# A second pool for the low parts of the weights, with 64 bytes ahead of those that stand as stationary operands

## The chip, the cores and the metric

One core of a Trainium2 chip runs the whole program in one launch. The metric is the device time of one execution in microseconds (us); less is better. Matrix products run on TensorE (PE in the rows; PEld is its loading of the stationary operand), evacuations and splits on VectorE (DVE) and ScalarE (ACT), transfers of weights are issued by SyncE (SP).

## The reference

One decoder layer on 256 tokens of 1024 channels in float32: a half-step SwiGLU block, a mixer (causal attention with 8 heads beside a short gated convolution, both from one input projection) and a second half-step SwiGLU block, each followed by a layer norm. Nearly all of the work is products of the 256 tokens with large weights.

```python
def swiglu(x, w_up, w_down):
    gate, up = jnp.split(x @ w_up, 2, axis=-1)          # w_up 1024 x 5632
    return (jax.nn.silu(gate) * up) @ w_down            # w_down 2816 x 1024

def hybrid_mixer(x, w_in, b_gate, conv_w, conv_b, w_proj_attn, w_proj_conv, w_out):
    z = x @ w_in                                        # w_in 1024 x 8192
    q, k, v, h, g_b, g_c, gates = jnp.split(z, SPLITS, axis=-1)
    y_attn = moba_attention(heads(q), heads(k), heads(v)) @ w_proj_attn
    y_conv = (g_b * short_conv(g_c * h, conv_w, conv_b)) @ w_proj_conv
    gate_attn, gate_conv = jnp.split(jax.nn.sigmoid(gates + b_gate), 2, axis=-1)
    return (gate_attn * y_attn + gate_conv * y_conv) @ w_out

def reference(x, ...):
    x = layer_norm(ALPHA * x + 0.5 * swiglu(x, ffn1_w_up, ffn1_w_down), ln1_g, ln1_b)
    x = layer_norm(ALPHA * x + hybrid_mixer(x, ...), ln2_g, ln2_b)
    return layer_norm(ALPHA * x + 0.5 * swiglu(x, ffn2_w_up, ffn2_w_down), ln3_g, ln3_b)
```

## The kernel before

**Three products for one.** Every operand is kept as two parts in the type fp32r: a high part (the value rounded to fp32r) and a low part (the rest). A product is high times high, plus high times low, plus low times high. All matmuls of this kind come from one helper and stand under L117; the shape tells them apart.

**Units of weights.** The weights come in units of 128 x 2048 elements (1 MB). SP loads a unit into one of three `raw` buffers, ScalarE writes its high part (L883) and VectorE its low part (L886) into two `S` buffers; there are ten of them, 8192 bytes per partition each, taken in turn. The function `prep` does this, and `advance` decides when, from planned times of use; `now["t"]` is that plan's clock, and nothing in it is measured. The q and k of the attention take `S` buffers too (one each for four heads), and `state["hold"]` keeps room for them.

**Two ways to multiply.** In `rows` and `D` the activations stand as the stationary operand (128 x 128) and 512 columns of weights move, high or low. In `cols` the weights stand and the activations (tiles `X`, transposed, high and low parts beside each other) move. One call of `cols` takes one unit (`col_unit`: 1024 rows by 256 columns of a weight) and issues 32 matmuls: 16 *wide* ones, with 128 x 128 of the high part standing and 512 columns moving (the high and low part of 256 tokens at once), and 16 *narrow* ones, with 128 x 128 of the low part standing and 256 columns moving (the high part alone). They stand in this order, for the two banks 0 and 1 of the unit:

```python
            wide.append(mm(lambda b=b: box[b], lambda c=c: u.hi[:, c], ... 512, u))
            narrow.append(mm(lambda b=b: box[b][:, 0:256], lambda c=c: u.lo[:, c], ... 256, u))
    return add(wide[:KT + 1] + narrow + wide[KT + 1:])      # 9 wide, 16 narrow, 7 wide
```

There are 74 such units: 20 of the first SwiGLU block's up projection, 28 of the input projection (q, k, gates, h, gc, gb), 8 of the two projections behind the mixers, 18 of the second SwiGLU block. So there are 1184 narrow matmuls with a weight's low part standing. The rest of TensorE's work is 2038 matmuls of 512 columns in fp32r (1184 of them the wide ones of `cols`), some hundred of attention, and transposes (L190).

**Order.** The whole program is recorded in one fixed order per engine; nothing is decided on the chip. Every tile of the program begins, within a partition, at a remainder of 128 bytes to a multiple of 512, but the `N` tiles (activations of 128 x 1032) and the small vectors: an `N` tile is 4128 bytes long, so that the nine of them begin at 0, 32, 64 or 96 bytes behind a multiple of 128 (the one of the transposes at the start of the second SwiGLU block's tokens 128 to 255 begins at 64).

Of the kernel before, what the change touches and what calls it, by code (L numbers as in the profile page):

```python
# [9 lines left out]
F = mybir.dt.float32  # L10
R = mybir.dt.float32r
# [15 lines left out]
LEAD, LEAD0, LEAD1, PACE, DELAY, QUIET = 30.0, -1.0, 0.9, 2.2, 1.2, 4.0  # L27
OFF, AT0, AT1, AT2, HEAD = 5.0, 1.3, 10.5, 15.0, 7.5
AD1, AD2, AD3 = 2.0, 1.5, 1.0
S_BUFS, X_BUFS, RAW_BUFS, N_BUFS, T_BUFS, ACC_BUFS = 10, 3, 3, 9, 8, 8  # L30


class Op:
# [6 lines left out]
class Unit:  # L40


    def __init__(self, src, chunks=2):
        self.src, self.chunks = src, chunks
        self.raw = self.hi = self.lo = None
        self.left = 0


class Slots:


    def __init__(self, pool, tag, shape, bufs):
        self.pool, self.tag, self.shape, self.bufs, self.live, self.n = pool, tag, shape, bufs, 0, 0

    def get(self, dt=F):
        assert self.live < self.bufs, self.tag
        self.live += 1
        self.n += 1
        return self.pool.tile(self.shape, dt, tag=self.tag, name=f"{self.tag}{self.n}", bufs=self.bufs)

    def free(self, n=1):
        self.live -= n
# [3 lines left out]
def layer(ctx: ExitStack, tc: tile.TileContext, a: dict, out: bass.AP):  # L66
# [3 lines left out]
    ctx.enter_context(tc.manual_schedule())  # L70

    S = Slots(sb, "S", [128, 2048], S_BUFS)
    X = Slots(sb, "X", [128, 4096], X_BUFS)
    RAW = Slots(sb, "raw", [128, 2048], RAW_BUFS)
    N = Slots(sb, "N", [128, 1032], N_BUFS)
# [2 lines left out]

    base, ins, units, sig, st = [], [], [], [], {}
    now = {"t": 0.0}  # L80
    state = {"dma": 0, "prep": 0, "chunk": 0, "t": -100.0, "hold": 0, "quiet": 0.0}


    for pool in (S, X, RAW, T):
        pool.get()
        pool.free()

# [46 lines left out]

    pending = []

    def new_unit(src, chunks=2):
        u = Unit(src, chunks)
        units.append(u)
        return u  # L140

# [36 lines left out]
    def col_unit(w, c0):  # L178

        return new_unit(lambda raw: [(raw.rearrange("p (k n) -> p k n", k=KT),  # L180
                                      w[:, c0:c0 + 256].rearrange("(k p) n -> p k n", p=128))])

    def transposes(src, n, evac):

# [364 lines left out]
    def QK(kind, c):  # L549
        def epi(bank, j):  # L550
            if j == 0:
                state["hold"] -= 1
                st[kind, c] = S.get(R).rearrange("p (s h n) -> p s h n", s=2, h=4)
            t_ = T.get()
            both(t_[:, 0:256], bank)
            split_later(st[kind, c][:, 0, j], st[kind, c][:, 1, j], t_[:, 0:256], T.free)

        return four(kind, c, epi)
# [61 lines left out]
    def attention(head, at, dt):  # L620
        c, h = head // 4, head % 4
        box = {}
        qT = lambda s, lo, hi: st["q", c][:, s, h, lo:hi]
        kT = lambda s, lo, hi: st["k", c][:, s, h, lo:hi]

        def bank(name, lo, hi):
            def f():
                if name not in box:
                    box[name] = ACC.get()
                return box[name][:, lo:hi]  # L630
            return f


        both_k = lambda: st["k", c][:, :, h, 0:128]
        ops = [mm(bank("S", 0, 256), lambda: qT(0, 0, 128), both_k, True, False, 256),
               mm(bank("S", 0, 128), lambda: qT(1, 0, 128), lambda: kT(0, 0, 128), False, True, 128)]
        ops += passes(bank("S", 256, 512), lambda s: qT(s, 128, 256), lambda w: kT(w, 0, 256), True, True, 256)

        def softmax():
            if head == 0:  # L640
                st["xT", "a"] = xnew()
            P = T.get()
            b = box["S"]
            mx = small([128, 2], "mx")
            sm = small([128, 2], "sm")
            nc.vector.scalar_tensor_tensor(P[:, 0:128], b[:, 0:128], SCALE, mask, op0=OP.mult, op1=OP.add)
            nc.vector.scalar_tensor_tensor(P[:, 0:128], b[:, 128:256], SCALE, P[:, 0:128], op0=OP.mult, op1=OP.add)
            nc.vector.tensor_scalar(P[:, 128:256], b[:, 256:384], SCALE, None, op0=OP.mult)
            nc.vector.scalar_tensor_tensor(P[:, 256:384], b[:, 384:512], SCALE, mask, op0=OP.mult, op1=OP.add)
            ACC.free()  # L650
            nc.vector.reduce_max(mx[:, 0:1], P[:, 0:128], axis=mybir.AxisListType.X)
            nc.vector.reduce_max(mx[:, 1:2], P[:, 128:384], axis=mybir.AxisListType.X)
            nc.vector.tensor_scalar(mx, mx, -1.0, None, op0=OP.mult)

            def exps():
                nc.scalar.activation(P[:, 0:128], P[:, 0:128], AF.Exp, bias=mx[:, 0:1], accum_out=sm[:, 0:1])
                nc.scalar.activation(P[:, 128:384], P[:, 128:384], AF.Exp, bias=mx[:, 1:2], accum_out=sm[:, 1:2])
                defer(AD2, recip)

            def recip():  # L660
                nc.vector.reciprocal(sm, sm)
                defer(AD3, norm)

            def norm():
                nc.scalar.activation(P[:, 0:128], P[:, 0:128], AF.Identity, scale=sm[:, 0:1])
                nc.scalar.activation(P[:, 128:384], P[:, 128:384], AF.Identity, scale=sm[:, 1:2])

            defer(AD1, exps)
            box["P"] = P

        ops[-1].after.append(softmax)
        put(at, dt, ops)

        def evac(tb):
            T.free()
            box["PT"] = [T.get(R)[:, 0:2 * n].rearrange("p (s n) -> p s n", s=2) for n in (256, 128)]
            for pt, c0, n in zip(box["PT"], (0, 256), (256, 128)):
                split(pt[:, 0], pt[:, 1], tb[:, c0:c0 + n])

        put(at, dt + AT1, transposes(lambda i: box["P"][:, i * 128:(i + 1) * 128], 3, evac))  # L680


        v = lambda s, kt: st["v"][:, s, kt, head * 128:(head + 1) * 128]
        flat = lambda i: box["PT"][i].rearrange("p s n -> p (s n)")
        late = lambda: bank("O", 0, 512)().rearrange("p (s n) -> p s n", s=2)[:, :, 128:256]
        ops = [mm(bank("O", 0, 512), lambda: v(0, 0), lambda: flat(0), True, False, 512),
               mm(late, lambda: v(0, 1), lambda: box["PT"][1], False, False, 256),
               mm(bank("O", 0, 256), lambda: v(1, 0), lambda: box["PT"][0][:, 0], False, False, 256),
               mm(bank("O", 128, 256), lambda: v(1, 1), lambda: box["PT"][1][:, 0], False, True, 128)]

        def fin():
            aT = st["xT", "a"][:, head].rearrange("p s t n -> p s (t n)")
            T.free(2)
            o = T.get()[:, 0:256]
            both(o, box["O"])
            ACC.free()
            split_later(aT[:, 0], aT[:, 1], o, T.free)
            if h == 3:
                S.free(2)
            if head == NH - 1:  # L700
                X.free()

        ops[-1].after.append(fin)
        put(at, dt + AT2, ops)

    def hold():
        state["hold"] += 2

    for t in range(2):
        for c in range(2):  # L710
# [166 lines left out]

    def prep(u, c):
        if c == 0:
            u.hi, u.lo = S.get(R), S.get(R)  # L880
        w = 2048 // u.chunks
        s = slice(c * w, (c + 1) * w)
        nc.scalar.copy(u.hi[:, s], u.raw[:, s])  # L883

        def rest():
            nc.vector.tensor_tensor(u.lo[:, s], u.raw[:, s], u.hi[:, s].bitcast(F), op=OP.subtract)  # L886
            if c == u.chunks - 1:
                RAW.free()

        defer(DELAY if now["t"] > 12 else 0.0, rest, u)  # L890
# [7 lines left out]
    def advance(must=None):  # L898
        flush(must)
        while state["prep"] < len(order):  # L900
            load()
            u, c, t = order[state["prep"]], state["chunk"], now["t"]
            if must is None or pos[id(must)] < state["prep"]:
                if need[id(u)] + c * 2.6 / u.chunks > t + min(LEAD, LEAD0 + t * LEAD1):
                    break
                if t < state["t"] + PACE * 2 / u.chunks * min(1, 0.4 + t * 0.03):
                    break
                if t < state["quiet"]:
                    break
                if c == 0 and S.live + state["hold"] + 2 > S_BUFS:  # L910
                    break
            prep(u, c)
            state["t"] = t
            state["chunk"] += 1
            if state["chunk"] == u.chunks:
                state["prep"] += 1
                state["chunk"] = 0
        flush(must)

    load()  # L920
    for t, op in zip(clock, prog):
# [3 lines left out]
        if op.unit is not None:  # L925
            op.unit.left -= 1
            if op.unit.left == 0:
                S.free(2)
        for f in op.after:
            f()  # L930
    now["t"] = 1e9
    flush()
    assert not any(s.live for s in (S, X, RAW, T, ACC, N)), [(s.tag, s.live) for s in (S, X, RAW, T, ACC, N)]


_INS = ["x", "ffn1_w_up", "ffn1_w_down", "ln1_g", "ln1_b", "w_in", "b_gate", "conv_w", "conv_b",
# [19 lines left out]
```

## Time and profile before

| | |
|---|---|
| time, median of 3 runs | 643.73 us (643.54 to 643.81) |
| time of the profiled execution | 643.73 us |
| its span (first to last instruction) | 642.0 us |
| TensorE busy | 633.2 us, 99% of the span |
| TensorE's loads of stationary operands | 547.7 us, 85% |
| VectorE busy | 455.7 us, 71% |
| ScalarE busy | 357.1 us, 56% |
| mean traffic with HBM | 188 GB/s |

The profiled execution took as long as the median run, and 1.73 us of it lie outside its span. The busy times overlap: each engine works on its own queue, and waits for others by semaphores. Matmuls are pipelined, so that the busy times of single matmuls overlap too: the length of one record (some 280 or 390 ns) is not its cost; the distance from one matmul's start to the next one's is.

### The profile page before, as it was taken

Reading aid. Unit: us, or ns where it says so; the run is one execution under the profiler, and the core shown is the slowest. Engines: PE = TensorE matmul, PEld = TensorE weight load, DVE = VectorE, ACT = ScalarE, POOL = GpSimd, SP = SyncE. Lnnn points to the kernel's source line nnn. Section 1 sums busy time; section 2 is a strip of 40 time slices with the busy share of each in tenths; the row PEclk is TensorE's granted clock in tenths of the full one; section 3 lists DMA queues with packets and bytes.
Section 4 is the critical chain, followed back from the end, with each engine's and each line's share of the span. In section 5 each row is a group of like instructions: output and inputs, shape, how many; then the busy total and the mean of one; then the engine's idle time right before and its main releaser. Section 6 shows DMA issues by size and latency. Waiting matters only on the chain.

```text
span 642.0 us, 8774 instructions
## 1 busy us (share of the span) xinstructions
PE 633.2 (99%) x3416; PEld 547.7 (85%) x3416; DVE 455.7 (71%) x732; ACT 357.1 (56%) x624; POOL 18.5 (3%) x25
## 2 busy tenths in 40 slices
PE   9999999999999999999999999999999999999995
PEld 6888888888888888898888888888888888888884
DVE  4786666666678577778869987886966676666627
ACT  5665555555534458676698665552556655555510
POOL 2000000000011000000000000001100000000001
PEclk9999999999999999999999999999999999999998
DMA  9865665667645572555666655572666756556301
GB/s 295 267 226 198 211 236 193 210 212 260 193 126 171 165 230 90 155 174 158 203 212 192 224 200 189 198 253 75 196 197 201 259 196 197 197 196 197 132 1 66
DMA packets 95854, 121.18 MB, mean 189 GB/s; under 512 B 2196, under 2 KB 84548, under 8 KB 95812
## 3 DMA queue, kind: packets, MB, share of 16 engines
q1 hardware_dynamic: 95524, 120.23, 57.6%
q8 instruction: 27, 0.44, 0.3%
q10 hardware_dynamic: 288, 0.39, 0.2%
q14 instruction: 15, 0.12, 0.1%
HBM read 119.56 MB, written 1.05 MB: 188 GB/s over the span
## 4 chain that ended last, share of the span: by engine, by line
PE 98%; DVE 1%; issue 0%; DVEq 0%; ACT 0%; POOL 0%; POOLq 0%
PE acc L117 96%; PE acc L190 1%; PE acc L147 0%; DVE N L824 0%; DVEq L952 0%; DVE S L886 0%; DVE N L828 0%; ACT X L203 0%; POOL T L90 0%; DVE bn L240 0%; DVE N L238 0%; DVE mv L250 0%; PE acc L719 0%; DVE X L204 0%; DVEq L886 0%
## 5 line engine op out<-in xcount | busy, mean ns | idle before, releaser
L117 PE MATMUL acc<-X,S 128*128 128x256 f32 (+1 forms) x2368 | 420.0, 338 | 0.0
L117 PEld LDWEIGHTS acc<-X,S 128*128 128x128 f32 x2368 | 363.4, 190 | 46.9
L886 DVE TENSOR_TENSOR S<-raw,S 128x1024 fp32r<-128x1024 f32 (+1 forms) x224 | 268.3, 1207 | 47.3 <-ACT S L883 46.0
L883 ACT CAST S<-raw 128x1024 fp32r<-128x1024 f32 (+1 forms) x224 | 227.7, 1034 | 47.6 <-PE acc L117 42.9
L117 PE MATMUL acc<-S,T 128*128 128x512 f32 (+1 forms) x546 | 123.4, 383 | 0.0
L117 PEld LDWEIGHTS acc<-S,T 128*128 128x128 f32 x546 | 100.1, 188 | 19.8
L379 DVE TENSOR_TENSOR T<-T,acc 128x256 f32<-128x256 f32 x132 | 55.4, 420 | 80.1 <-ACT T L378 79.7
L378 ACT COPY T<-acc 128x256 f32<-128x256 f32 x132 | 49.0, 371 | 99.1 <-PE acc L117 99.1
L117 PE MATMUL acc<-S,X 128*128 128x512 f32 x336 | 80.4, 395 | 0.1
L117 PEld LDWEIGHTS acc<-S,X 128*128 128x128 f32 x336 | 62.3, 188 | 13.7 <-DVE S L886 0.7
L213 ACT CAST T<-T 128x256 fp32r<-128x256 f32 x38 | 15.5, 407 | 24.9 <-DVE T L430 24.6
L424 ACT ACTIVATE T<-T 128x256 f32<-128x256 f32 x38 | 15.9, 418 | 13.9 <-DVE T L379 13.9
L203 ACT CAST X<-acc 128x512 fp32r<-128x512 f32 x16 | 9.4, 588 | 22.7 <-PE acc L190 14.3
L252 POOL TENSOR_TENSOR rs<-mv,mhalf 128x1 f32<-128x1 f32 x6 | 6.2, 1036 | 459.7 <-DVE mv L250 459.7
L204 DVE TENSOR_TENSOR X<-acc,X 128x512 fp32r<-128x512 f32 x16 | 10.9, 687 | 12.0 <-ACT X L203 11.9
L238 DVE SCALAR_TENSOR_TENSOR N<-acc,N 128x512 f32<-128x512 f32 (+1 forms) x13 | 8.4, 646 | 15.2 <-PE acc L117 15.2
L208 DVE TENSOR_TENSOR T<-T,T 128x256 fp32r<-128x256 f32 x38 | 15.9, 419 | 1.9 <-ACT T L213 1.9
L430 DVE TENSOR_TENSOR T<-T 128x256 f32<-128x256 f32 x38 | 16.2, 425 | 1.3
L203 ACT CAST T<-acc 128x128 fp32r<-128x128 f32 (+1 forms) x28 | 8.2, 293 | 15.1 <-DVE T L204 13.7
L379 DVE TENSOR_TENSOR N<-N,acc 128x256 f32<-128x256 f32 x24 | 10.0, 416 | 5.6 <-ACT N L378 5.6
L213 ACT CAST X<-T 128x256 fp32r<-128x256 f32 x16 | 6.5, 407 | 12.1 <-DVE T L379 6.8
L204 DVE TENSOR_TENSOR T<-acc,T 128x128 fp32r<-128x128 f32 (+1 forms) x28 | 9.1, 327 | 5.4 <-ACT T L203 5.4
(70 smaller groups left out, 213.8 us busy)
## 6 DMA issues: line engine op xcount, KB each, us to landing
raw<-in_ffn_w_up SPq DMA_DIRECT2D x38, 1024.0 KB, 5.1
raw<-in_w_in SPq DMA_DIRECT2D x32, 1024.0 KB, 5.4
raw<-in_ffn_w_down SPq DMA_DIRECT2D x22, 1024.0 KB, 4.8
raw<-in_w_proj_attn SPq DMA_DIRECT2D x4, 1024.0 KB, 5.3
raw<-in_w_proj_conv SPq DMA_DIRECT2D x4, 1024.0 KB, 4.9
raw<-in_w_out SPq DMA_DIRECT2D x4, 1024.0 KB, 5.0
raw<-in_ffn_w_up SPq DMA_DIRECT2D x8, 512.0 KB, 4.8
raw<-in_ffn_w_up SPq DMA_DIRECT2D x8, 256.0 KB, 5.3
```

Of the source, the lines that this page charges most:

```text
L117: return Op(lambda: nc.tensor.matmul(dst(), lhsT=lhsT(), rhs=rhs(), start=start, stop=stop), cols, unit)
L203: nc.scalar.copy(hi, src)
L204: nc.vector.tensor_tensor(lo, src, hi.bitcast(F), op=OP.subtract)
L208: nc.vector.tensor_tensor(lo, src, hi.bitcast(F), op=OP.subtract)
L213: nc.scalar.copy(hi, src)
L238: nc.vector.scalar_tensor_tensor(y[:, c], src, scale, st["ax", t][:, c], op0=OP.mult, op1=OP.add)
L378: nc.scalar.copy(dst, bank[:, 256:512])
L379: nc.vector.tensor_tensor(dst, dst, bank[:, 0:256], op=OP.add)
L424: defer(0.8, lambda: nc.scalar.activation(g[:, 0:256], g[:, 0:256], AF.Silu))
L430: nc.vector.tensor_tensor(g[:, 0:256], g[:, 0:256], g[:, 256:512], op=OP.mult)
L883: nc.scalar.copy(u.hi[:, s], u.raw[:, s])
L886: nc.vector.tensor_tensor(u.lo[:, s], u.raw[:, s], u.hi[:, s].bitcast(F), op=OP.subtract)
```

## The change

The `S` buffers are divided: high parts (and q) stay in `S`, now with five buffers, and low parts (and k) go to a new pool `L` with five. An `L` buffer has 32 elements (128 bytes) more than an `S` buffer, and the low part of a unit from `col_unit` begins 16 elements (64 bytes) behind its start; other low parts, and k, begin at the start. The counts of held buffers are kept for q and k apart.

```diff
-S_BUFS, X_BUFS, RAW_BUFS, N_BUFS, T_BUFS, ACC_BUFS = 10, 3, 3, 9, 8, 8
+S_BUFS, X_BUFS, RAW_BUFS, N_BUFS, T_BUFS, ACC_BUFS = 5, 3, 3, 9, 8, 8
...
-    def __init__(self, src, chunks=2):
-        self.src, self.chunks = src, chunks
+    def __init__(self, src, chunks=2, skip=0):
+        self.src, self.chunks, self.skip = src, chunks, skip
...
-    def get(self, dt=F):
-        assert self.live < self.bufs, self.tag
+        self.room = room
+
+    def get(self, dt=F, skip=0):
+        assert self.live < self.bufs and skip <= self.room, self.tag
         self.live += 1
         self.n += 1
-        return self.pool.tile(self.shape, dt, tag=self.tag, name=f"{self.tag}{self.n}", bufs=self.bufs)
+        p, n = self.shape
+        t = self.pool.tile([p, n + self.room], dt, tag=self.tag, name=f"{self.tag}{self.n}", bufs=self.bufs)
+        return t[:, skip:skip + n] if self.room else t
...
     S = Slots(sb, "S", [128, 2048], S_BUFS)
+    L = Slots(sb, "L", [128, 2048], S_BUFS, 32)
...
         return new_unit(lambda raw: [(raw.rearrange("p (k n) -> p k n", k=KT),
-                                      w[:, c0:c0 + 256].rearrange("(k p) n -> p k n", p=128))])
+                                      w[:, c0:c0 + 256].rearrange("(k p) n -> p k n", p=128))], skip=16)
...
-                st[kind, c] = S.get(R).rearrange("p (s h n) -> p s h n", s=2, h=4)
+                st[kind, c] = (S if kind == "q" else L).get(R).rearrange("p (s h n) -> p s h n", s=2, h=4)
...
-            u.hi, u.lo = S.get(R), S.get(R)
+            u.hi, u.lo = S.get(R), L.get(R, u.skip)
...
-                if c == 0 and S.live + state["hold"] + 2 > S_BUFS:
+                if c == 0 and max(S.live + state["holdq"], L.live + state["holdk"]) >= S_BUFS:
```

No instruction is added, removed or moved: on every engine the same instructions stand in the same order with the same shapes (lines are ten further down, and buffer numbers one higher). TensorE's queue at one unit of the first SwiGLU block, before (`S_790` is the unit's high part, `S_791` its low part, `X_115` the activations, `acc` the two banks):

```order
L117 MATMUL acc_922<-X_115,S_790 128x512 x8
L117 MATMUL acc_932<-X_115,S_790 128x512
L117 MATMUL acc_922<-X_115,S_791 128x256 x8
L117 MATMUL acc_932<-X_115,S_791 128x256 x8
L117 MATMUL acc_932<-X_115,S_790 128x512 x7
```

The same place with the change:

```order
L127 MATMUL acc_923<-X_116,S_791 128x512 x8
L127 MATMUL acc_933<-X_116,S_791 128x512
L127 MATMUL acc_923<-X_116,L_792 128x256 x8
L127 MATMUL acc_933<-X_116,L_792 128x256 x8
L127 MATMUL acc_933<-X_116,S_791 128x512 x7
```

Only the buffer that the sixteen narrow matmuls load their stationary operand from has moved, to another address.

By the addresses of the two built programs, the low parts of `col_unit` begin at a remainder of 0 (before) and of 64 (after) to 128 bytes. Since `L` buffers are longer, everything behind them lies 640 bytes further: `X`, `T` and `raw` keep their remainder to 128, while against the `S` buffers, whose addresses stay, they are displaced by 128 to a multiple of 512; the five `L` buffers lie at 0, 128, 256 and 384 to it.

## Rows read from the trace of the kernel before

**Rows 1.** The page, part 1: engine, busy us, share, instructions.

```profile
PE 633.2 (99%) x3416; PEld 547.7 (85%) x3416; DVE 455.7 (71%) x732; ACT 357.1 (56%) x624; POOL 18.5 (3%) x25
```

**Rows 2.** TensorE's waits: engine, line, releaser: total us, times, longest us.

```profile
PE acc L147 <- POOL T L90: 1.3, 1, 1.3
```

**Rows 3.** TensorE's groups by shape, whole span: count | busy us, mean ns | idle.

```profile
L117 PE MATMUL acc<-X,S 128*128 128x512 f32 x1184 | 288.9, 392 | 0.0
L117 PE MATMUL acc<-X,S 128*128 128x256 f32 x1184 | 154.7, 283 | 0.0
L117 PE MATMUL acc<-S,T 128*128 128x512 f32 x510 | 119.1, 390 | 0.0
L117 PE MATMUL acc<-S,X 128*128 128x512 f32 x336 | 80.4, 395 | 0.1
```

**Rows 4.** Timeline around one unit: wide, narrow, next wide (start, length, count).

```profile
97.54 1.98 PE L117 MATMUL acc<-X,S 128*128 128x512 f32 x8
...
99.82 1.48 PE L117 MATMUL acc<-X,S 128*128 128x256 f32 x11
...
101.26 1.55 PE L117 MATMUL acc<-X,S 128*128 128x512 f32 x6
```

**Rows 5.** That unit's groups: first narrow, wides behind, wides ahead; loads for wides, narrows.

```profile
L117 PE MATMUL acc<-X,S 128*128 128x256 f32 x1 | 0.3, 277 | 0.0
...
L117 PE MATMUL acc<-X,S 128*128 128x512 f32 x2 | 0.6, 396 | 0.0
...
L117 PE MATMUL acc<-X,S 128*128 128x512 f32 x9 | 2.2, 389 | 0.0
...
L117 PEld LDWEIGHTS acc<-X,S 128*128 128x128 f32 x10 | 1.9, 188 | 0.4
...
L117 PEld LDWEIGHTS acc<-X,S 128*128 128x128 f32 x13 | 1.6, 192 | 0.0
```

**Rows 6.** Timeline: three narrow matmuls behind an attention step.

```profile
240.16 0.52 PE L117 MATMUL acc<-X,S 128*128 128x256 f32 x3
```

**Rows 7.** Timeline: transposes of an N tile and of a T tile; then their group.

```profile
458.87 0.60 PE L190 MATMUL acc<-ident,N 128*128 128x128 f32 x4
...
251.32 0.49 PE L190 MATMUL acc<-ident,T 128*128 128x128 f32 x3
...
L190 PE MATMUL acc<-ident,T 128*128 128x128 f32 x36 | 6.2, 272 | 0.0
```

**Rows 8.** Groups of the split on ScalarE and VectorE, with what ended their idle time.

```profile
L883 ACT CAST S<-raw 128x1024 fp32r<-128x1024 f32 x216 | 222.9, 1049 | 45.8 <-PE acc L117 42.9 <-DMA raw<-in_ffn_w_up 2.5 <-DMA raw<-in_w_in 0.4
...
L886 DVE TENSOR_TENSOR S<-raw,S 128x1024 fp32r<-128x1024 f32 x216 | 262.6, 1224 | 45.8 <-ACT S L883 44.6
```

**Rows 9.** Span and granted clock.

```profile
core 0: 642.0 us, clock 0.997
```

More of the change, by code (lines that the diff above doesn't have):

```diff
@@ L49, with __init__ @@
 class Slots:
-    def __init__(self, pool, tag, shape, bufs):
+    def __init__(self, pool, tag, shape, bufs, room=0):
         self.pool, self.tag, self.shape, self.bufs, self.live, self.n = pool, tag, shape, bufs, 0, 0
-    def get(self, dt=F):
-        assert self.live < self.bufs, self.tag
+        self.room = room
+    def get(self, dt=F, skip=0):
+        assert self.live < self.bufs and skip <= self.room, self.tag
         self.live += 1
         self.n += 1
-        return self.pool.tile(self.shape, dt, tag=self.tag, name=f"{self.tag}{self.n}", bufs=self.bufs)
+        p, n = self.shape
+        t = self.pool.tile([p, n + self.room], dt, tag=self.tag, name=f"{self.tag}{self.n}", bufs=self.bufs)
+        return t[:, skip:skip + n] if self.room else t
     def free(self, n=1):
@@ L80, in layer @@
     now = {"t": 0.0}
-    state = {"dma": 0, "prep": 0, "chunk": 0, "t": -100.0, "hold": 0, "quiet": 0.0}
-    for pool in (S, X, RAW, T):
+    state = {"dma": 0, "prep": 0, "chunk": 0, "t": -100.0, "holdq": 0, "holdk": 0, "quiet": 0.0}
+    for pool in (S, L, X, RAW, T):
         pool.get()
@@ L135, in layer, with new_unit @@
     pending = []
-    def new_unit(src, chunks=2):
-        u = Unit(src, chunks)
+    def new_unit(src, chunks=2, skip=0):
+        u = Unit(src, chunks, skip)
         units.append(u)
@@ L551, in epi @@
             if j == 0:
-                state["hold"] -= 1
-                st[kind, c] = S.get(R).rearrange("p (s h n) -> p s h n", s=2, h=4)
+                state["hold" + kind] -= 1
+                st[kind, c] = (S if kind == "q" else L).get(R).rearrange("p (s h n) -> p s h n", s=2, h=4)
             t_ = T.get()
@@ L698, in fin @@
             if h == 3:
-                S.free(2)
+                S.free()
+                L.free()
             if head == NH - 1:
@@ L706, in hold @@
     def hold():
-        state["hold"] += 2
+        state["holdq"] += 1
+        state["holdk"] += 1
     for t in range(2):
@@ L927, in layer @@
             if op.unit.left == 0:
-                S.free(2)
+                S.free()
+                L.free()
         for f in op.after:
@@ L932, in layer @@
     flush()
-    assert not any(s.live for s in (S, X, RAW, T, ACC, N)), [(s.tag, s.live) for s in (S, X, RAW, T, ACC, N)]
+    assert not any(s.live for s in (S, L, X, RAW, T, ACC, N)), [(s.tag, s.live) for s in (S, L, X, RAW, T, ACC, N)]
 _INS = ["x", "ffn1_w_up", "ffn1_w_down", "ln1_g", "ln1_b", "w_in", "b_gate", "conv_w", "conv_b",
```

## The prediction

> **What bounds the kernel now.** I read the page's busy times first: TensorE 99% of the span, everything else at 85% or less [rows 1]. A busy TensorE may still be one that waits between busy stretches, so the waits came next: all of its waits for other engines sum to 1.3 us, one wait at the very start [rows 2]. The granted clock is 0.997 over the span, so TensorE ran at its upper level of 2.4 GHz nearly throughout [rows 9]. What is left is the matmul stream itself: the time is the sum of the distances between starts, and only something that changes a distance changes the time.
>
> So I took the distances from the timeline, where a row gives a start, a length and a count: the length less the last record's own length, over the count less one. Eight wide matmuls ahead of a unit's narrow ones: (1.98 − 0.39) / 7 = 0.227 us. Eleven narrow ones: (1.48 − 0.28) / 10 = 0.120 us [rows 3, 4]. Their difference, 107 ns, is 256 columns at 2.4 GHz (256 / 2.4 = 106.7), so the columns stream at full rate. Twice that is 213 ns, and what a wide matmul takes beyond is 13 to 14 ns; a narrow one takes 13 ns beyond its 107. Each matmul pays a fixed 13 ns whatever its shape. On a narrow one that is 11% of its distance, and 1184 x 13 = 15.4 us in the whole program. That is the stake of this change, and its ceiling.
>
> Is the 13 ns fixed, or does part of it come from where the operands lie? The groups of one unit say something. The first narrow matmul, which stands behind a wide one, has a record of 277 ns; the mean of all 1184 is 283 [rows 3, 5]. The loads of stationary operands for wide matmuls take 188 ns, those for narrow ones in mid-run 192 [rows 5]. And the first wides behind the narrow run have records of 396 ns against 389 ahead of it [rows 5], and a distance of (1.55 − 0.39) / 5 = 0.232 us [rows 4]. So in the narrow run the moving stream and the load beside it are both longer than each is elsewhere, by 6 and 4 ns. Nothing else is different there: same engine, same tiles, same clock. Behind an attention step, three narrow matmuls go by at (0.52 − 0.28) / 2 = 0.12 us too [rows 6]; the two-digit row leaves room for 116 to 121 ns. I read the 6 ns as two streams that get in each other's way while the load of the next low part runs beside the moving operand; a stall of one 64-byte piece (16 float32 columns at 2.4 GHz) would be 6.7 ns, which fits the 6 and is an inference from its size.
>
> **The change part by part.**
>
> The pools. Order, shapes and counts are the same on every engine, SP's and the DMA's included, so no wait is added by position. Five and five buffers in turn hold as many units as ten did, and in both built programs the first write to a buffer stands behind the last matmul that reads its former content by the same number of matmuls (at the tightest places two, in the middle some twenty). ScalarE's split waits for TensorE in 42.9 of its 45.8 us of idle time, VectorE's for ScalarE's half in 44.6 [rows 8]: both follow TensorE and have room (56% and 71% busy [rows 1]), so if TensorE gets some 1% faster they follow. The cost is nothing, covered by that room; without it, a split is 1049 + 1224 ns per half unit [rows 8] and would show as a wait of TensorE for L886.
>
> The 640 bytes by which `X` and `T` move against `S`. They keep their place to 128 bytes and change it to 256 and 512. Before, all operands of these matmuls have the same place to 512, so the trace has no row with another and can't price it. The three kinds of 512-column matmuls, with high parts, low parts, `X` or `T` on either side, have means of 392, 390 and 395 ns [rows 3], all at one alignment. I take nothing, and bound it from both sides by the 6 ns that a record is seen to vary (389 and 396 [rows 5]): for 2038 such matmuls that would be 12 us either way, so I give it a chance of its own below and don't add it.
>
> The 64 bytes. They touch the stationary operand of 1184 matmuls and nothing else on TensorE. If the collision hangs on whether both streams start in the same half of 128 bytes, then moving one of them by half of it takes the stall away where it stands now. By the records: 283 − 277 = 6 ns for 15 of the 16 narrow matmuls of a unit, and about as much (396 − 390) for the first wide one behind: 16 x 6 = 96 ns a unit, times 74 units = 7.1 us. The rest of the slow wides behind a narrow run ((0.232 − 0.227) x 5 = 25 ns a unit, 1.9 us in all, of which 0.4 is in the 7.1) I leave where it is, since nothing shows which of the two streams they stem from. VectorE's writes of the low part move by 64 bytes as well; they are contiguous as before, and off the path.
>
> Sum, against the profiled execution's own time, which equals the median: 643.7 − 7.1 = **636.6 us**.
>
> A rule speaks against it. The Trainium skill, in "SBUF — State Buffer", section "SBUF: two separate sides", and in "TensorE: Matmul & The Clock Gate", step 1 of its step-by-step section, gives TensorE two independent read ports and says that loading the next weights takes nothing from the running matmul; by that the sum would be 643.7. The records of 192 against 188 and 283 against 277 ns disagree with it, if only by a few ns. The same page's back-to-back gap is the columns over 2.4 GHz and 2.5 ns more; by that a narrow matmul would take 109 ns, and the sum with all 1184 there is an estimate of 643.7 − 1184 x 0.011 = 631.
>
> **The rivals.**
>
> *No change, 643.7.* The 13 ns belong to every matmul of the type, the 6 ns are a matter of when a record begins, and addresses don't matter. For it: the 13 ns are equal on the wide ones, where high parts, `X` and `T` stand. And the only rows with another alignment show nothing: four transposes whose `N` tile begins 64 bytes behind a multiple of 128 go by at (0.60 − 0.27) / 3 = 0.110 us, three with an aligned `T` tile at (0.49 − 0.27) / 2 = 0.110 [rows 7]. Against it: a transpose takes 110 ns for 128 columns, twice the time per column of the others, so its streams have room that those of a narrow matmul lack; and sixteen equal matmuls whose first has a shorter record than the next fifteen speak for something that builds up between neighbours. This is also the case in which the change does nothing.
>
> *Slower, 650.8.* The mechanism is the same with the sign turned. The loads beside wide matmuls (188 ns) show that at the present alignment there are phases without a collision; the 64 bytes could put the narrow run's into a worse one, with a second stall of 6 ns per matmul: +7.1 us. It decides as soon as narrow matmuls stand more than 120 ns apart. For it: matmuls and loads of the same alignment are seen both with and without the stall, so the phase counts beside the address, and the first narrow matmul, now free, could be the one that is hit. Against it: a run settles at one distance, and the present one is already a stalled one.
>
> *Half of it, about 640.* The run settles in a phase between, 3 ns better (117 instead of 120 ns): 1184 x 3 = 3.6 us. [rows 6] leaves room for such a phase.
>
> *More, about 630.* The whole 13 ns go (643.7 − 15.4 = 628.3), or the displaced `X` and `T` free the wides too (half of the 12 us: 631).
>
> **How the numbers follow.** Chances: 0.36 for the forecast (634 to 639), 0.14 for half of it, 0.10 for more, 0.22 for no change, 0.18 for slower. Faster by over 0.2% (1.3 us, about what a measurement of this kernel can tell from none): 0.60; within: 0.22; slower: 0.18. The likeliest is 636.6. The range reaches up over "no change" to 644.6 and down to 631, which leaves out the slower case and a small part of "more", 2 in 10 together; if the change works at all, its own range is 631 to 641.
>
> **What would show it.** Right: narrow rows of the timeline at 113 to 115 ns apart instead of 120, their group's mean at 277 to 279 instead of 283, the loads in a narrow run at 188, wide groups unchanged at 390 to 395, and the same waits. Wrong in a step: narrow at 120 and loads at 192 (addresses don't matter); narrow over 120 and loads longer (slower); wide groups moved by some ns (the 640 bytes count, not only the 64); a wait of TensorE for L886 (the pools count). The prediction would be wrong above all if the 6 ns are no collision at all.

## The result

The changed kernel is slower: 648.6 us (median of 4 runs, 648.59 to 648.95) against 643.7 us, a ratio of 1.0077 with a 95% interval of 1.0064 to 1.009. The forecast was 636.6 us, with a range of 631 to 644.6.

The page of the changed kernel, part 1, shows the same engines at the same load; TensorE alone is busy longer, by as much as the span has grown (642.0 to 646.8 us; [rows 1]):

```profile
span 646.8 us, 8786 instructions
...
PE 637.9 (99%) x3416; PEld 544.7 (84%) x3416; DVE 455.3 (70%) x732; ACT 356.9 (55%) x624; POOL 18.5 (3%) x25
```

Its waits are a third of a microsecond longer in all, so the pools' turn isn't it [rows 2]:

```profile
PE acc L157 <- POOL T L100: 1.3, 1, 1.3
PE acc L127 <- DVE L L898: 0.3, 1, 0.3
```

TensorE's groups by shape in the changed kernel (count | us in which the group is busy, mean ns of one record):

```profile
L127 PE MATMUL acc<-X,S 128*128 128x512 f32 x1184 | 293.4, 395 | 0.0
L127 PE MATMUL acc<-X,L 128*128 128x256 f32 x1184 | 151.4, 279 | 0.0
L127 PE MATMUL acc<-S,T 128*128 128x512 f32 x340 | 109.3, 394 | 0.0
L127 PE MATMUL acc<-S,X 128*128 128x512 f32 x224 | 71.9, 397 | 0.0
L127 PE MATMUL acc<-L,T 128*128 128x512 f32 x170 | 66.9, 394 | 0.0
L127 PE MATMUL acc<-L,X 128*128 128x512 f32 x112 | 44.5, 398 | 0.3 <-DVE L L898 0.3
```

The narrow group did what was forecast in kind: 283 to 279 ns, 154.7 to 151.4 us [rows 3]. But every wide group has grown by 3 to 5 ns, those too that have nothing to do with `cols`: the wide ones of `cols` from 288.9 to 293.4 us, those with a `T` tile standing from 390 to 394 ns. (Here the groups of `S` and `L` are apart, in [rows 3] they were one; their busy times are compared below with a kernel that has both pools.)

The timeline of the unit of [rows 4] in the changed kernel (start, length, count): seven wides ahead, fifteen narrow ones, five wides behind:

```profile
98.12 1.79 PE L127 MATMUL acc<-X,S 128*128 128x512 f32 x7
...
100.10 1.93 PE L127 MATMUL acc<-X,L 128*128 128x256 f32 x15
...
101.86 1.33 PE L127 MATMUL acc<-X,S 128*128 128x512 f32 x5
```

The wides are (1.79 − 0.39) / 6 = 0.233 us apart where they were 0.227, the narrow ones (1.93 − 0.28) / 14 = 0.118 where they were 0.120. A narrow matmul gains 2 ns, and a wide one loses 5 to 6.

Not every narrow run of this kernel is like that one. A run of another unit, whose operands lie at the same distance to each other by the built program's addresses, goes by at (1.86 − 0.28) / 14 = 0.113 us:

```profile
66.71 1.86 PE L127 MATMUL acc<-X,L 128*128 128x256 f32 x15
```

Of the 69 units whose 16 narrow matmuls stand together, 20 settle at 113 ns in this kernel and 49 at 118.

### The profile page after: what moved, and what is told of

It is laid out like the page before. It is cut to its first block, busy times and chain, and to the rows that moved or that the text cites. A ratio compares the mean times of both kernels' runs of the same rounds, so it can differ in the third digit from the quotient of the medians.

```text
span 646.8 us, 8786 instructions
## 1 busy us (share of the span) xinstructions
PE 637.9 (99%) x3416; PEld 544.7 (84%) x3416; DVE 455.3 (70%) x732; ACT 356.9 (55%) x624; POOL 18.5 (3%) x25
## 4 chain that ended last, share of the span: by engine, by line
PE 98%; DVE 1%; issue 0%; DVEq 0%; ACT 0%; POOL 0%; POOLq 0%
PE acc L127 96%; PE acc L200 1%; PE acc L157 0%; DVE N L836 0%; DVEq L965 0%; DVE L L898 0%; DVE N L840 0%; ACT X L213 0%; POOL T L100 0%; DVE bn L250 0%; DVE N L248 0%; DVE mv L260 0%; PE acc L731 0%; DVE X L214 0%; DVEq L898 0%
## 5 line engine op out<-in xcount | busy, mean ns | idle before, releaser
L898 DVE TENSOR_TENSOR L<-raw,S 128x1024 fp32r<-128x1024 f32 (+1 forms) x224 | 267.7, 1205 | 50.4 <-ACT S L895 49.3
L127 PE MATMUL acc<-X,S 128*128 128x512 f32 x1184 | 293.4, 395 | 0.0
L127 PEld LDWEIGHTS acc<-X,S 128*128 128x128 f32 x1184 | 216.4, 188 | 45.0
L127 PEld LDWEIGHTS acc<-X,L 128*128 128x128 f32 x1184 | 149.0, 188 | 6.3
L127 PE MATMUL acc<-X,L 128*128 128x256 f32 x1184 | 151.4, 279 | 0.0
L127 PEld LDWEIGHTS acc<-S,T 128*128 128x128 f32 x364 | 67.6, 188 | 14.8
L127 PE MATMUL acc<-L,T 128*128 128x512 f32 (+1 forms) x182 | 70.3, 386 | 0.0
L127 PE MATMUL acc<-L,X 128*128 128x512 f32 x112 | 44.5, 398 | 0.3 <-DVE L L898 0.3
L127 PEld LDWEIGHTS acc<-L,T 128*128 128x128 f32 x182 | 34.2, 188 | 7.5
L127 PEld LDWEIGHTS acc<-L,X 128*128 128x128 f32 x112 | 21.1, 188 | 5.1 <-DVE L L898 0.6
```

The costliest lines, as they stand in the source:

```text
L127: return Op(lambda: nc.tensor.matmul(dst(), lhsT=lhsT(), rhs=rhs(), start=start, stop=stop), cols, unit)
```

## The experiments

Two theories stood at the start. One: the 640 bytes by which `X`, `T` and `raw` moved against `S` slow the wide matmuls, whatever the low parts do. The other: the 64 bytes themselves slow the wide ones beside the narrow ones. In the diffs a "pool" line is the fourth argument of `L` (elements that a buffer is longer), and `skip` is the low part's beginning in elements.

**The pools alone.**

```diff
-    L = Slots(sb, "L", [128, 2048], S_BUFS, 32)
+    L = Slots(sb, "L", [128, 2048], S_BUFS, 0)
...
-                                      w[:, c0:c0 + 256].rearrange("(k p) n -> p k n", p=128))], skip=16)
+                                      w[:, c0:c0 + 256].rearrange("(k p) n -> p k n", p=128))], skip=0)
```

> Two pools of five, no longer L buffers and no 64 bytes: every operand has the address alignment of the kernel before. All address theories: 643.7, same groups. Rival (the pools' turn costs waits): up to 648.

643.59 us, ratio 0.9996 (0.9986 to 1.0005). The pools cost nothing. Its groups are the ones to compare with, since names and order are those of the changed kernel:

```profile
L127 PE MATMUL acc<-X,S 128*128 128x512 f32 x1184 | 288.9, 392 | 0.0
L127 PE MATMUL acc<-X,L 128*128 128x256 f32 x1184 | 154.6, 283 | 0.0
L127 PE MATMUL acc<-S,T 128*128 128x512 f32 x340 | 107.7, 389 | 0.0
L127 PE MATMUL acc<-S,X 128*128 128x512 f32 x224 | 71.1, 393 | 0.5 <-ACT S L895 0.5
L127 PE MATMUL acc<-L,T 128*128 128x512 f32 x170 | 66.2, 390 | 0.0
L127 PE MATMUL acc<-L,X 128*128 128x512 f32 x112 | 44.2, 394 | 0.3 <-DVE L L898 0.3
```

Against these, the changed kernel's groups are longer by 4.5 (X,S wide), 1.6 + 0.7 (with `T`) and 0.8 + 0.3 (with `X` standing), and shorter by 3.2 (narrow): +4.7 us in sum, of the 5.0 between the two kernels. The whole loss is in the wide matmuls.

**The displacement alone.** The pool line as in the change, `skip` 0.

> The change with its longer L buffers, but no 64 bytes: low parts begin at the buffer's start, X and T stay displaced by 128 bytes to a multiple of 256. Theory (the displacement is what costs): wide groups as in the changed kernel, 394 to 398 ns, narrow ones near the old 283, since the low part and X differ by a multiple of 128: 643.7 + 8 = about 652. Rival (the 64 bytes slow the neighbours): 643.7.

651.14 us, ratio 1.0117 (1.0102 to 1.0132): 7.5 us slower than the pools alone. Four of its groups:

```profile
L127 PE MATMUL acc<-X,S 128*128 128x512 f32 x1184 | 293.4, 395 | 0.0
L127 PE MATMUL acc<-X,L 128*128 128x256 f32 x1184 | 153.8, 282 | 0.0
L127 PE MATMUL acc<-S,T 128*128 128x512 f32 x340 | 109.3, 394 | 0.0
L127 PE MATMUL acc<-S,X 128*128 128x512 f32 x224 | 72.2, 398 | 0.0
```

The wide groups are those of the changed kernel. The second theory falls: the wides lose without any 64 bytes. The run holds a check on the place within itself, since the five `L` buffers lie at different places. Of the low parts that move past a standing `T` tile (`L,T`), 53 lie at its place to 256 by the built program's addresses: their records have a mean of 391 ns. The other 116 lie 128 bytes off, and theirs have 394.

**The 64 bytes alone.** Buffers of `L` are 256 bytes longer instead of 128, so `X`, `T` and `raw` lie 1280 bytes further than in the kernel before, five times 256, and an `L` buffer begins at 128 or 384 to a multiple of 512.

```diff
-    L = Slots(sb, "L", [128, 2048], S_BUFS, 32)
+    L = Slots(sb, "L", [128, 2048], S_BUFS, 64)
```

> The change as it is, but each L buffer 256 bytes longer instead of 128, so that X, T, raw and the L buffers keep their place to 256 bytes against S; the low parts of col units still begin 64 bytes behind. If the loss came from the displacement by 128 bytes (theory), the wide groups go back from 395 to 392 ns and the S,T ones from 394 to 390, the narrow ones keep their 279, and the time is 643.7 - 3.4 = about 640.3. If the 64 bytes themselves slow the wide matmuls that stand beside the narrow ones (rival), the S,T group goes back but the X,S group stays at 395, and the time is about 644. If the pools cost it (rival), it stays at 648.6.

641.86 us, ratio 0.9968 (0.9957 to 0.998): faster than both kernels, by 1.9 us over the one before. Its first two groups and the same unit's timeline, wides ahead and narrow ones:

```profile
L127 PE MATMUL acc<-X,S 128*128 128x512 f32 x1184 | 288.8, 392 | 0.0
L127 PE MATMUL acc<-X,L 128*128 128x256 f32 x1184 | 152.4, 281 | 0.0
```

```profile
97.32 1.75 PE L127 MATMUL acc<-X,S 128*128 128x512 f32 x7
...
99.25 1.93 PE L127 MATMUL acc<-X,L 128*128 128x256 f32 x15
```

The wides are back at (1.75 − 0.39) / 6 = 0.227 us, and the narrow group gives back 2.2 us. The displacement by 1280 bytes, a multiple of 256, costs nothing; the one by 640, 128 beyond such a multiple, costs 7.5 us. And the 64 bytes are worth 1.9 us and not the 3.4 that were expected here, nor the 7.1 of the prediction.

**Everything 64 bytes further.** A tile of 64 bytes ahead of `S`, nothing else against the pools alone.

```diff
-    for pool in (S, L, X, RAW, T):
+    for pool, pad in ((S, 16), (L, 0), (X, 0), (RAW, 0), (T, 0)):
+        if pad:
+            sb.tile([128, pad], F, name=f"pad{pool.tag}")
         pool.get()
```

> A tile of 64 bytes ahead of all others and nothing else: S, L, X, T and raw all begin 64 bytes further, with the same distances as in the kernel before. If only the distance between the moving and the standing operand counts (theory): 643.7, wide 227 ns, narrow 120 ns apart. If the place itself counts (rival: 64 bytes behind a multiple of 128 is good or bad for an operand by itself): narrow ones near 117 and a time some 2 us away.

643.75 us, ratio 1.0001 (0.9992 to 1.001), narrow rows as before:

```profile
99.74 1.96 PE L129 MATMUL acc<-X,L 128*128 128x256 f32 x15
```

Moving all operands together by 64 bytes changes nothing, while moving one against the other does: it is the distance between the standing and the moving operand's places that counts in these runs. Other common shifts were not run.

**Other places of `X`.** The activations begin 64, 192 or 32 bytes behind, by stage (`X` buffers are 256 bytes longer; `L` is as in the pools alone).

```diff
-    X = Slots(sb, "X", [128, 4096], X_BUFS)
+    X = Slots(sb, "X", [128, 4096], X_BUFS, 64)
...
-    def xnew():
-        return X.get(R).rearrange("p (k s t n) -> p k s t n", k=KT, s=2, t=2)
+    def xnew(key):
+        return X.get(R, {'x': 16, 'm': 48, 'f': 8}.get(key, 0)).rearrange("p (k s t n) -> p k s t n", k=KT, s=2, t=2)
```

> Two pools, all weights aligned as before, but the activations X begin 64 bytes behind their buffer in the first SwiGLU block, 192 bytes behind in the input projection, 32 bytes behind in the second SwiGLU block, and 0 elsewhere; T as before. A look at the dose: if only the distance between the two operands' places to 256 bytes counts, narrow matmuls of the first block and of the input projection go to some 116 to 117 ns (from 120), since X 64 behind is the low part 192 behind. What wide matmuls do at these distances no run shows yet; if they lose as at 128 bytes (5 ns each, 1500 of them) the time is near 643.7 + 7 - 3 = 648, if 64 bytes free them as they free the narrow ones it is near 643.7 - 3 - 5 = 636.

645.12 us, ratio 1.0022 (1.0013 to 1.0031), between the two sums expected: the narrow ones gain and the wides lose. One unit of the input projection, where both parts of the weight begin 64 bytes behind `X`'s place to 256, wides and then narrow ones; and the wides of a unit of the first block, where they begin 192 bytes behind it:

```profile
344.67 1.79 PE L127 MATMUL acc<-X,S 128*128 128x512 f32 x7
...
346.65 1.86 PE L127 MATMUL acc<-X,L 128*128 128x256 f32 x15
...
97.47 1.77 PE L127 MATMUL acc<-X,S 128*128 128x512 f32 x7
```

In the first unit the wides are (1.79 − 0.39) / 6 = 0.233 us apart and the narrow ones (1.86 − 0.28) / 14 = 0.113; in the second the wides are at 0.230. With the 64 bytes alone, where the low part has the same distance to `X` but the high part none, the narrow ones are at 0.118 (above). So a narrow run's distance doesn't hang on its own operands' places alone: what ran ahead of it counts too.

Nor is it only the places of what ran ahead. With the 64 bytes alone, where all units have the same places to 256, a run that stands behind two wides after an attention step goes by at (1.75 − 0.28) / 13 = 0.113 us, against the 0.118 above:

```profile
239.55 1.75 PE L127 MATMUL acc<-X,L 128*128 128x256 f32 x14
```

A run keeps the distance that it settles at, and at one and the same place there are runs at 113 and at 118 ns.

**A scan of the high part's place.** From unit to unit the high part begins 16 bytes further, 0 to 240, low part and all else at equal places (to 256; the `S` buffers are 256 bytes longer, the `L` buffers as in the pools alone).

```diff
+        u.skip = 4 * (state["cols"] % 16) if skip else 0
+        state["cols"] += bool(skip)
...
-            u.hi, u.lo = S.get(R), L.get(R, u.skip)
+            u.hi, u.lo = S.get(R, u.skip), L.get(R)
```

> The same scan for the high part: it begins 0 to 240 bytes behind from unit to unit in steps of 16, and the low part and all else stay at equal places. A dose curve for the wide matmuls: 227 ns at 0 and 232 at 128 are known. If 0 is the best place, nearly all units lose up to 16 x 6 = 96 ns, and the time is about 643.7 + 74 x 0.09 = 650; if some place is better than 0, it shows there, and a faster kernel follows from it.

647.08 us, ratio 1.0057 (1.0034 to 1.008), less than the 650 expected. Seven wides of the units with the high part 0, 32, 96 and 192 bytes behind `X`, in this order:

```profile
147.88 1.75 PE L127 MATMUL acc<-X,S 128*128 128x512 f32 x7
...
30.98 1.79 PE L127 MATMUL acc<-X,S 128*128 128x512 f32 x7
...
64.39 1.80 PE L127 MATMUL acc<-X,S 128*128 128x512 f32 x7
...
114.51 1.77 PE L127 MATMUL acc<-X,S 128*128 128x512 f32 x7
```

At 0 they are 0.227 us apart, and in the first unit of each of the fifteen other places 0.230 to 0.235. One place is better than its first unit, which runs near the program's start: in its later units 16 bytes is as good as 0, (1.98 − 0.39) / 7 = 0.227:

```profile
153.22 1.98 PE L127 MATMUL acc<-X,S 128*128 128x512 f32 x8
```

For the wide matmuls ahead of a narrow run no place tried is better than equal places. Here only the high parts changed their place to 256 bytes, so that the wides lose without `X`, `T` or `raw` being displaced.

**A scan of the low part's place,** in steps of 16 bytes with the high part at equal places. Its edit is that of the scan above for `u.skip`, with `L` buffers 256 bytes longer, and `L.get(R, u.skip)` as in the change.

> As the 64-byte shift alone (256 bytes more per L buffer, nothing displaced), but the low part's beginning goes from unit to unit in 16 steps of 16 bytes, 0 to 240. A dose curve for the narrow matmuls, with the wide ones all at equal places: at 0 they should stand 120 ns apart, at 64 about 117. If the stall hangs on halves of 128 bytes, the curve has two levels; if on 256 bytes, a period of 256; the wide ones stay at 227. The time is near 641.5.

642.8 us, ratio 0.9986 (0.9975 to 0.9997). Fifteen narrow matmuls of the units at 0, 64, 80, 112 and 208:

```profile
148.75 1.96 PE L127 MATMUL acc<-X,L 128*128 128x256 f32 x15
...
49.51 1.93 PE L127 MATMUL acc<-X,L 128*128 128x256 f32 x15
...
55.06 1.94 PE L127 MATMUL acc<-X,L 128*128 128x256 f32 x15
...
71.62 1.96 PE L127 MATMUL acc<-X,L 128*128 128x256 f32 x15
...
121.32 1.91 PE L127 MATMUL acc<-X,L 128*128 128x256 f32 x15
```

This is no curve of two levels by halves of 128 bytes, since 112 behaves like 0 and 208 is better than 64; and it has no period of 128, since 80 and 208 differ.

**208 bytes for all units** (`skip=52` on the 64 bytes alone).

> Nothing displaced, and the low parts of col units 208 bytes behind instead of 64: in the scan the sixteen narrow matmuls and the six wide ones behind them took 3010 ns at 208, 3047 at 64 and 3073 at 0. If that holds for all 74 units: 643.7 - 74 x 0.063 = 639.0. If the scan's gain hung on the neighbours with other places, about 641.8 as with 64 bytes.

639.91 us, ratio 0.9939 (0.9925 to 0.9952). The scan's order carries over, with 3.8 of the 4.7 us.

**A finer scan,** 180 to 240 bytes in steps of 4.

> The scan of the low part's beginning in steps of 4 bytes, from 180 to 240. If pieces of 16 bytes count, places within one piece give the same time and 208 to 220 is the best step; if the single element counts, each place differs. Near 640.5.

642.93 us, ratio 0.9987 (0.9976 to 0.9997), more than the 640.5 expected. Fifteen narrow matmuls at 180, and at 192 to 224 in steps of 4:

```profile
149.13 1.87 PE L127 MATMUL acc<-X,L 128*128 128x256 f32 x15
...
38.83 1.93 PE L127 MATMUL acc<-X,L 128*128 128x256 f32 x15
...
49.84 1.94 PE L127 MATMUL acc<-X,L 128*128 128x256 f32 x15
...
55.37 1.96 PE L127 MATMUL acc<-X,L 128*128 128x256 f32 x15
...
66.37 2.01 PE L127 MATMUL acc<-X,L 128*128 128x256 f32 x15
...
72.00 1.91 PE L127 MATMUL acc<-X,L 128*128 128x256 f32 x15
...
82.95 1.92 PE L127 MATMUL acc<-X,L 128*128 128x256 f32 x15
...
88.46 1.95 PE L127 MATMUL acc<-X,L 128*128 128x256 f32 x15
...
99.49 1.98 PE L127 MATMUL acc<-X,L 128*128 128x256 f32 x15
...
105.08 1.91 PE L127 MATMUL acc<-X,L 128*128 128x256 f32 x15
```

One element more, from 204 to 208, and a run is 100 ns shorter. Pieces of 64 bytes don't explain that, since both places lie in one. Places within a piece of 16 bytes don't give the same time either: from 192 to 204 and from 208 to 220 the runs grow longer. But both falls, at 208 and at 224, lie at multiples of 16, so such pieces are not ruled out as a part of the cause.

**The best and the worst place of that scan** for all units (`skip=45` and `skip=51`).

> The best place of the fine scan, 180 bytes, for all 74 units: 2988 ns there against 3073 for sixteen narrow matmuls and six wide ones behind them, so 643.7 - 74 x 0.085 = 637.4, with narrow matmuls mostly 113 ns apart. If the scan's order can't be carried over, somewhere between 640 and 644.

> The worst place of the fine scan, 204 bytes, 24 bytes from the best one: 3125 ns against 3073, so 643.7 + 74 x 0.052 = 647.5. If places within a 16-byte or 64-byte piece do the same, it is near 640 to 643.

638.72 us, ratio 0.9921 (0.9907 to 0.9936), against 637.4 expected, and 647.38 us, ratio 1.0056 (1.0039 to 1.0073), against 647.5. The narrow groups of the first and of the second:

```profile
L127 PE MATMUL acc<-X,L 128*128 128x256 f32 x1184 | 149.2, 278 | 0.0
```

```profile
L127 PE MATMUL acc<-X,L 128*128 128x256 f32 x1184 | 157.8, 285 | 0.0
```

The two kernels differ by 24 bytes in where the low parts begin, and by 8.7 us; 157.8 − 149.2 = 8.6 us of it is in the narrow group. 638.72 us is the fastest of all: 4.9 us under the kernel before, 9.9 us under the changed one.

At 204 bytes, too, the place doesn't settle a run alone. An ordinary run, and one behind two wides after an attention step:

```profile
99.89 2.01 PE L127 MATMUL acc<-X,L 128*128 128x256 f32 x15
...
253.52 1.75 PE L127 MATMUL acc<-X,L 128*128 128x256 f32 x14
```

The first goes by at (2.01 − 0.28) / 14 = 0.124 us, the second at (1.75 − 0.28) / 13 = 0.113.

## Why the prediction was wrong

**The step that failed: "The 640 bytes by which `X` and `T` move against `S`. ... I take nothing".** It was bounded at 12 us either way, priced at nothing and given a part of a chance of 0.10, and only as a gain. The displacement alone costs 7.5 us: wide matmuls whose operands lie 128 bytes apart to a multiple of 256 take some 5 ns more, and there are 2038 of them (5 x 2038 = 10 us if each paid it in full). The prediction's own remark, that all operands before had one place to 512 and so the trace could say nothing of another, was the reason to keep the upper bound in the range. A term that touches 2038 matmuls was left at zero beside one that touches 1184 and was worked out to the nanosecond.

**The term of the 64 bytes: right in sign, mis-sized.** −7.1 us was forecast, −1.9 us measured alone. The mechanism was taken from the first narrow matmul's record, 277 against 283 ns [rows 3, 5]. With 64 bytes most runs settle not at 113 ns but at 118. At 180 bytes they do settle lower ((1.87 − 0.28) / 14 = 0.114), so most of the 6 ns can be had, but not reliably at the place that the change chose. Even there it isn't 7.1 us: the narrow group is 5.4 us shorter than with the pools alone (154.6 to 149.2), and the kernel 4.9. The part of the term that stood for the first wide matmul behind a run (396 − 390, where its rows have 389) did not come with the 64 bytes alone: their wide group takes 288.8 us, against 288.9 before. Of the rivals "half of it" comes nearest to this term: it had 117 ns, though also 3.6 us.

**The rule of two ports.** The Trainium skill ("TensorE: Matmul & The Clock Gate", step 1 of its step-by-step section) has the loading of the next weights take nothing from the running matmul. The prediction read from it that the sum would stay at 643.7, so that no place would matter; here places do matter for these fp32r matmuls: from 180 to 204 bytes, the same 1184 matmuls take 149.2 or 157.8 us. Whether it is the loading that takes this time from the matmuls, no run shows.

**The rival "slower" had the sign and not the cause.** It had a second stall on the narrow matmuls, at more than 120 ns apart. In the changed kernel they stand at 118 or 113. Runs beyond 120 ns do exist, at 204 bytes, where most stand at (2.01 − 0.28) / 14 = 0.124.

**What held.** The distances between starts bound the kernel: in all thirteen kernels the span is longer than TensorE's busy time by 8.7 to 9.7 us. The pools cost nothing (643.59 us). ScalarE and VectorE followed a faster TensorE without becoming the bound: in the fastest kernel it waits 0.8 us for them. The signs named for the narrow group came in part: its mean is 279 ns and the loads beside it take 188 in the changed kernel (191 with the pools alone).

**The sum.** −1.9 for the 64 bytes and +7.5 for the displacement give +5.6 alone, and +4.9 was measured together; the remainder is in the narrow group, which has 151.4 us in the changed kernel and 152.4 with the 64 bytes alone: of the units whose 16 narrow matmuls stand together, 20 settle at 113 ns in the first and four in the second.

**What stays open.** That the collision is one between the moving stream and the load of the next stationary operand is an inference: what is shown is that the distance of the two places counts, and that a common shift of 64 bytes doesn't. The loads shortened to 189 ns with the displacement alone as well, where the narrow group gained only 0.8 us. Why 180 is good and 204 bad, and why a run settles at 113 in one unit and at 118 or 124 in another with the same places, no run explains; the prediction's picture of 64-byte pieces and halves of 128 bytes is refuted by the scans. Places below 180 were tried in steps of 16 bytes only, so a better one than 180 may exist.

## What to carry to other kernels

A longer buffer moves everything that is allocated behind it: when a change shifts one operand on purpose, list the places of all others to 256 bytes, before and after, and pad so that those that shouldn't move keep them. Where matmuls with alternating stationary operands are the bound, the distance between the two operands' places is worth a scan from unit to unit in one run, since one profile then shows all places side by side; the place found is then to be tried in all units, since a run's distance hangs also on what ran ahead of it (208 bytes kept 3.8 of the 4.7 us). A side effect that the trace has no row for, on more instructions than the intended effect, belongs in the range at its bound.

## What the runs showed of the hardware

For fp32r matmuls of 128 x 128 standing and 512 or 256 columns moving, at the 2.4 GHz level (granted clock 0.996 to 0.998), the distance between starts depends on where the two operands lie to each other: 0.227 us (512 columns, ahead of a narrow run) at equal places and up to 0.235 elsewhere; 0.120 us (256 columns) at equal places, between 0.113 and 0.124 elsewhere, with a jump of 7 ns from one 4-byte place to the next (204 to 208). The best place differs by shape: equal places for 512 columns, 180 bytes of those tried for 256. Equal matmuls with the same distance of places stood 0.118 or 0.113 us apart at 64 bytes, and 0.124 or 0.113 at 204, depending on what ran ahead of them.
